# Block-diagonal gate products with the weight rows moving, turned back by transposes, in a two-layer hybrid block

## The chip, the cores and the metric

The kernel runs on one NeuronCore of a Trainium2 chip. The metric is the device time of one execution in microseconds (us). TensorE (PE in the rows, its weight loads PEld) multiplies, VectorE (DVE), ScalarE (ACT) and GpSimd (POOL) do the elementwise work, and SyncE (SP) issues the loads. A measurement is a set of executions on one chip, and its median is compared with that of the kernel before on the same chip.

## The reference, cut to what matters

A block of 256 tokens and width 2048 goes through a first layer (recurrence, attention, feed-forward, gated embedding) and two layers of a second kind. The change lies in the recurrence of the first layer:

```
D_RNN = 2816; N_RNN_BLOCKS = 16; RNN_BLOCK = 176
xb = x.reshape(B, S, N_RNN_BLOCKS, RNN_BLOCK)
r = sigmoid(einsum('bsnc,ncd->bsnd', xb, w_a).reshape(B, S, D_RNN) + b_a)
i = sigmoid(einsum('bsnc,ncd->bsnd', xb, w_x).reshape(B, S, D_RNN) + b_x)
log_a = -8 * r * softplus(-lam)
u = sqrt(-expm1(2 * log_a)) * (i * x)
h[t] = exp(log_a)[t] * h[t-1] + u[t]
```

Here x is the result of a causal convolution of width 4 over a projection of the input. The two gates r and i need a product with a block-diagonal matrix each: 16 blocks of 176x176. The chip works on 128 rows at a time, so the blocks do not fall on its boundaries.

## The kernel before, in words

All activations lie transposed: 128 features on the partitions, 256 tokens along the row. D_RNN is 22 such chunks ("m" in the code). All products are in float32 made of two float32r parts, a high and a low one: high times high, high times low, low times high.

**Weights.** All weights come from one stream, in tiles of eight 128x128 chunks (`G = 8`), in the order in which the program asks for them (`wnext`). `prep` issues a tile's load on SP, ScalarE copies its high part (`whi`, line 98 by way of `act`), VectorE subtracts for the low part (`wlo`, line 196). Four tiles of each part are held, so weights are prepared three tiles ahead (`LA = 3`).

**A projection** (`proj`, `mm3`) is 16 chunks of 128 input rows. The weight chunk is the stationary operand, the 256 tokens move; high and low part of the activation stand side by side, so a chunk is one matmul of 512 columns and one of 256 (lines 217, 218). `joined` adds the halves up: a ScalarE copy, then VectorE.

**The stage of the change.** A loop over m makes the projection for the recurrence (`xr_job`, with the convolution and its split into high and low part) and for its gelu gate (`gr_job`). When enough chunks are there, `rg_job` makes the two gate products of one output chunk: for both matrices, over the two to four input chunks that `rg_span` gives (70 in all for the 22 output chunks), three matmuls of 256 columns (lines 220 to 222): 22 jobs, 70 x 2 x 3 = 420 matmuls. Both gates share one PSUM bank of 512 columns (`pm`, tag "mm", four banks), which one ScalarE copy brings to SBUF. The weights come as zero-padded 128x128 chunks of the block-diagonal matrix. Four output chunks at a time go through `lru`: eight steps of pointwise work (sigmoid, tanh, exp, gelu, root, scan), queued as `sides`, of which the loop takes one after each projection or job. Behind the loop come the projections of a further gate (`gate_job`, m = 1 to 15), `flush` for steps that are left, and the product with `w_rnn_out`, which needs all 22 results.

**What sets the order.** TensorE's instructions run in the order in which the program writes them. A scheduler orders the other engines' instructions when the program is built; on each engine they then run strictly in that order, and an instruction that waits holds up those behind it. PSUM has eight banks: four with tag "mm", two "at" (`pa`), two "st" (`pst`). The tile `cs` holds constants, the identity among them, which line 810 to 812's transposes in a later layer use; it is loaded by line 560.

## Time and profile before

| | |
|---|---|
| median of 3 runs | 2869.33 us (2869.13 to 2869.34) |
| the profiled execution's own time | 2869.06 us |
| its span in the profile | 2866.9 us |
| granted TensorE clock, mean | 0.998 of full speed |

The span runs from the first to the last instruction; some 2 us around it belong to the execution's own time. "Busy" counts the time in which an engine has an instruction; matmuls overlap, so the distance from one start to the next is the price of a matmul, not its duration. A group of instructions is shown with its count, its busy time, the mean duration in ns, and the idle time of its engine just before it with what ended that. A timeline row has start, duration, engine, line, operation, output and inputs; `c`, `w` and `x` are tiles in SBUF, `pm`, `pa` and `pst` banks of PSUM, `raw` a weight tile as loaded.

### The profile page before, as it was taken

To read this page: it belongs to the slowest core of one execution; us is meant where nothing else is said; L and a number is where in the kernel's file an instruction comes from. 1 tells how busy PE (TensorE), PEld (TensorE's weight loads), DVE (VectorE), ACT (ScalarE), POOL (GpSimd) and SP (SyncE) were. 2 spreads that over 40 slices of the span, in tenths; PEclk is the share of its full clock that TensorE was granted. 3 is DMA by queue.
4 is the path that set the end of the run, shared out by engine and by line. 5 is a ranking of instruction groups with operands and counts; after the bars stand their busy time and mean duration, and the time that the engine had idled before them with its cause. 6 is when DMAs were issued, how large, how long until landed. Compare 5 with 4: busy or idle time off the path is not lost.

```text
span 2866.9 us, 43239 instructions
## 1 busy us (share of the span) xinstructions
PE 2846.1 (99%) x16414; PEld 2496.8 (87%) x16414; DVE 2018.1 (70%) x3306; ACT 1645.0 (57%) x2628; POOL 136.8 (5%) x155
## 2 busy tenths in 40 slices
PE   9999999999999999999999999999999999999997
PEld 8988888888888888888888888888888889888886
DVE  8788765666665776566565666776795688896676
ACT  6778764677765555544445455555464656554654
POOL 0112100111110000000000000000000001000000
PEclk9999999999999999999999999999999999999999
DMA  7565555545455556555555555655555555545553
GB/s 250 179 199 180 196 190 185 184 165 166 163 175 180 188 191 217 188 187 191 186 189 189 190 190 185 211 186 191 177 169 169 176 189 173 193 158 176 170 185 124
DMA packets 146433, 527.04 MB, mean 184 GB/s; under 512 B 16708, under 2 KB 17244, under 8 KB 146224
## 3 DMA queue, kind: packets, MB, share of 16 engines
q1 hardware_dynamic: 144720, 520.00, 54.8%
q0 software_dynamic: 1504, 4.29, 0.4%
q8 instruction: 128, 2.10, 0.3%
q14 instruction: 81, 0.66, 0.1%
HBM read 522.10 MB, written 4.47 MB: 184 GB/s over the span
## 4 chain that ended last, share of the span: by engine, by line
PE 99%; DVE 1%; DMA 0%; ACT 0%; SPq 0%; issue 0%; DVEq 0%
PE pm L217 55%; PE pm L218 28%; PE pm L290 3%; PE pm L289 3%; PE pm L291 3%; PE pm L221 2%; PE pm L220 2%; PE pm L222 2%; PE pa L795 0%; PE pa L819 0%; PE pa L598 0%; PE pa L796 0%; PE pa L619 0%; DVE x L1122 0%; DMA x<-xin_dram 0%; PE pa L217 0%
## 5 line engine op out<-in xcount | busy, mean ns | idle before, releaser
L217 PE MATMUL pm<-c,whi 128*128 128x512 f32 x6778 | 2382.6, 395 | 1.6 <-DVE c L355 1.6
L218 PE MATMUL pm<-c,wlo 128*128 128x256 f32 x6778 | 1898.5, 280 | 0.1
L196 DVE TENSOR_TENSOR wlo<-raw,whi 128x1024 fp32r<-128x1024 f32 (+1 forms) x984 | 1203.8, 1224 | 783.3 <-ACT whi L98 777.4
L98 ACT ACTIVATE whi<-raw 128x1024 fp32r<-128x1024 f32 (+1 forms) x984 | 1039.4, 1057 | 967.4 <-PE pm L217 500.4
L217 PEld LDWEIGHTS pm<-c,whi 128*128 128x128 f32 x6778 | 1273.1, 188 | 294.5 <-DVE c L355 1.9
L218 PEld LDWEIGHTS pm<-c,wlo 128*128 128x128 f32 x6778 | 1275.6, 188 | 0.8 <-DVE wlo L196 0.4
L98 ACT ACTIVATE c<-pm 128x256 f32<-128x256 f32 (+1 forms) x376 | 150.5, 402 | 110.7 <-PE pm L218 106.4
L98 ACT ACTIVATE c<-c 128x256 fp32r<-128x256 f32 (+2 forms) x357 | 139.2, 408 | 46.6 <-DVE c L450 24.9
L228 DVE TENSOR_TENSOR c<-pm,c 128x256 f32<-128x256 f32 x338 | 141.1, 418 | 4.5 <-ACT c L98 4.5
L289 PE MATMUL pm<-whi,c 128*128 128x512 f32 x320 | 126.9, 396 | 0.0
L290 PE MATMUL pm<-wlo,c 128*128 128x512 f32 x320 | 126.3, 395 | 0.0
L291 PE MATMUL pm<-whi,c 128*128 128x512 f32 x320 | 126.1, 394 | 0.0
L909 DVE SCALAR_TENSOR_TENSOR c<-w,sv,c 128x256 f32<-128x256 f32 x240 | 109.4, 497 | 0.8
L221 PE MATMUL pm<-c,whi 128*128 128x256 f32 (+1 forms) x377 | 106.4, 282 | 0.0
L220 PE MATMUL pm<-c,whi 128*128 128x256 f32 (+1 forms) x377 | 106.3, 282 | 0.0
L222 PE MATMUL pm<-c,wlo 128*128 128x256 f32 (+1 forms) x377 | 106.0, 281 | 0.0
L104 ACT ACTIVATE c<-c 128x256 f32<-128x256 f32 x219 | 85.5, 407 | 16.0 <-DVE c L228 14.1
L230 DVE TENSOR_TENSOR c<-c,c 128x256 f32<-128x256 f32 x176 | 75.8, 431 | 4.2
L291 PEld LDWEIGHTS pm<-whi,c 128*128 128x128 f32 x320 | 60.1, 188 | 14.2
L289 PEld LDWEIGHTS pm<-whi,c 128*128 128x128 f32 x320 | 60.1, 188 | 13.7
L290 PEld LDWEIGHTS pm<-wlo,c 128*128 128x128 f32 x320 | 60.1, 188 | 13.5
L220 PEld LDWEIGHTS pm<-c,whi 128*128 128x128 f32 x377 | 70.9, 188 | 0.9
(245 smaller groups left out, 1570.5 us busy)
## 6 DMA issues: line engine op xcount, KB each, us to landing
raw<-wst_dram SPq DMA_DIRECT2D x980, 512.0 KB, 3.3
scratch<-rows POOLq DMA_DIRECT2D x1, 2304.0 KB, 17.7
out_dram<-x SPq DMA_DIRECT2D x8, 256.0 KB, 2.0
x<-xin_dram SPq DMA_DIRECT2D x6, 256.0 KB, 7.7
c<-scratch POOLq DMA_DIRECT2D x12, 128.0 KB, 3.8
raw<-wst_dram SPq DMA_DIRECT2D x4, 256.0 KB, 4.0
sv<-vec_dram SPq DMA_DIRECT2D x1, 538.0 KB, 9.0
x<-xin_dram SPq DMA_DIRECT2D x4, 128.0 KB, 3.8
```

The lines of the kernel that those rows point to most:

```text
L98: return S.activation(o, i, func, **kw)
L196: V.tensor_tensor(lo[:, s], raw[:, s], h[:, s].bitcast(F32), op=OP.subtract)
L217: PE.matmul(o, wh, a[:, 0:512], start=first, stop=False)
L218: PE.matmul(o[:, 256:512], wl, a[:, 0:256], start=False, stop=last)
L220: PE.matmul(o, wh, a[:, 0:n], start=first, stop=False)
L221: PE.matmul(o, wh, a[:, n:2 * n], start=False, stop=False)
L222: PE.matmul(o, wl, a[:, 0:n], start=False, stop=last)
L228: V.tensor_tensor(t, o[:, 0:256], t, op=OP.add)
L289: PE.matmul(o, ah[:, tb], wh, start=first, stop=False)
L290: PE.matmul(o, ah[:, tb], wl, start=False, stop=False)
L291: PE.matmul(o, al[:, tb], wh, start=False, stop=last)
L909: V.scalar_tensor_tensor(a, pad[:, k:k + 256], wcol, a, op0=OP.mult, op1=OP.add)
```

## The change

The two gates' rows of one block now stand side by side as 352 columns and are the moving operand; the activation is the stationary one, in two halves of 128 tokens. `rg_block` works on one block of 176 instead of one output chunk of 128: for each of the two or three input chunks that the block touches, and for both token halves, three matmuls of 352 columns into two banks of tag "st". The result has tokens on the partitions. ScalarE copies it, cut at the boundaries of the 128-feature chunks, into one tile per chunk (`side_by`). `rg_turn` then turns a chunk back with four 128x128 transposes on TensorE (two gates, two token halves) into one bank of tag "at", and one ScalarE copy of 512 columns brings it to SBUF as before. A turn comes behind the next projection after its block. The constants with the identity are loaded with the vectors near the start; the gate projection m = 1 is put ahead of the last turns; the weight stream gets three-chunk requests that never cross a tile, with unused chunks where they would (7856 instead of 7852 chunks, 982 tiles of eight both times).

```diff
     def late_loads():
+        nc.sync.dma_start(cs, cst[:, :640])
         nc.sync.dma_start(sv, vec)
...
-    def rg_job(m):
-        span = rg_span(m)
-        both = pm(512)
-        for j, (key, d) in enumerate((("rg_a", rt), ("rg_x", it))):
-            proj(key, m, [xcs[k] for k in span], span, o=both[:, j * 256:(j + 1) * 256])
+    def rg_block(b):
+        span = block_span(b)
+        os = [pst(512) for _ in range(2)]
+        for kr in span:
+            ah, al = hl(xcs[kr])
+            wh, wl = (w[:, 0:2 * RNN_BLOCK] for w in wnext("rg", kr, b, 3))
+            first, last = kr == span[0], kr == span[-1]
+            for h, o in enumerate(os):
+                tb = slice(h * 128, (h + 1) * 128)
+                PE.matmul(o[:, 0:2 * RNN_BLOCK], ah[:, tb], wh, start=first, stop=False)
+                PE.matmul(o[:, 0:2 * RNN_BLOCK], ah[:, tb], wl, start=False, stop=False)
+                PE.matmul(o[:, 0:2 * RNN_BLOCK], al[:, tb], wh, start=False, stop=last)
+        for m in span:
+            if m not in side_by:
+                side_by[m] = slot()
+            lo, hi = max(b * RNN_BLOCK, m * 128), min((b + 1) * RNN_BLOCK, (m + 1) * 128)
+            to = side_by[m].rearrange("p (a h f) -> p a h f", a=2, h=2)
+            for h, o in enumerate(os):
+                with tc.high_priority():
+                    act(to[:, :, h, lo - m * 128:hi - m * 128],
+                        o[:, 0:2 * RNN_BLOCK].rearrange("p (a f) -> p a f", a=2)[:, :, lo - b * RNN_BLOCK:hi - b * RNN_BLOCK],
+                        AF.Copy)
...
+    def rg_turn(m):
+        s = side_by.pop(m)
+        both = pa(512)
+        for j in range(4):
+            PE.transpose(both[:, j * 128:(j + 1) * 128], s[:, j * 128:(j + 1) * 128], ident)
         t = slot()
         rt[m], it[m] = t[:, 0:256], t[:, 256:512]
         with tc.high_priority():
             act(t, both, AF.Copy)
...
     for m in range(KR):
         xr_job(m)
         side()
+        turn_to(ready)
         gr_job(m)
         side()
         if m == KR - 1:
             gate_job(0, COL_GA)
             side()
-        while ready < KR and rg_span(ready)[-1] <= m - min(2 if m < 4 else 1, KR - 1 - m):
-            rg_job(ready)
+        turn_to(ready)
+        while done < N_BLOCKS and block_span(done)[-1] <= m - min(2 if m < 4 else 1, KR - 1 - m):
+            rg_block(done)
             side()
...
+            done += 1
+        ready = KR if done == N_BLOCKS else done * RNN_BLOCK // 128
+    gate_job(1, COL_GA)
+    turn_to(KR)
+    order.extend([None] * (-len(order) % G))
...
-    for m in range(1, KD):
+    for m in range(2, KD):
         gate_job(m, COL_GA)
         side()
     flush()
...
-    nc.sync.dma_start(cs, cst[:, :640])
```

`turn_to(n)` turns the chunks up to n and queues `lru` for every four of them.

In the rows of the order that follow, the changed kernel's lines have their own numbers (L477 to L479 are the block products, L497 the transposes, L99 and L105 what L98 and L104 were).

**Order on TensorE, the seam of the last products.** Before, where the job of output chunk 19 ends and that of 20 begins (`pm_3437` and `pm_3470` are their banks, `c_` the split activation):

```order
L221 MATMUL pm_3437<-c_3142,whi_3377 128x256
L222 MATMUL pm_3437<-c_3142,wlo_3378 128x256
L220 MATMUL pm_3470<-c_3016,whi_3377 128x256 [waits PE_49]
L221 MATMUL pm_3470<-c_3016,whi_3377 128x256
L222 MATMUL pm_3470<-c_3016,wlo_3378 128x256
```

Now, where block 14 ends and block 15 begins (`pst_3452` and `pst_3453` are block 14's banks, `pst_3477` and `pst_3478` block 15's, in the same two places of PSUM):

```order
L479 MATMUL pst_3452<-whi_3384,c_3164 128x352
L477 MATMUL pst_3453<-whi_3384,c_3164 128x352
L478 MATMUL pst_3453<-wlo_3385,c_3164 128x352
L479 MATMUL pst_3453<-whi_3384,c_3164 128x352
L477 MATMUL pst_3477<-whi_3410,c_3164 128x352 [waits PE_49,Activation_49]
L478 MATMUL pst_3477<-wlo_3411,c_3164 128x352 [waits DVE_49]
L479 MATMUL pst_3477<-whi_3410,c_3164 128x352
L477 MATMUL pst_3478<-whi_3410,c_3164 128x352 [waits PE_49,Activation_49]
```

The products now wait for ScalarE at both of block 15's banks, which they did not at the seam before.

**Order on ScalarE, the same place.** Before, the copies of the jobs of chunks 19 to 21 out of their banks:

```order
L98 ACTIVATE c_3468<-pm_3437 128x512 [waits PE_49]
L104 ACTIVATE c_3468<-c_3468,sv 128x256 [waits Activation_49]
L104 ACTIVATE c_3468<-c_3468,sv 128x256
L98 ACTIVATE whi_3499<-raw_3497 128x1024 [waits DMAHW5_49,DVE_49,PE_49]
L98 ACTIVATE c_3489<-pm_3470 128x512 [waits PE_49,Pool_49]
L98 ACTIVATE c_3515<-pm_3496 128x512 [waits PE_49]
```

Now, the copies out of block 14's two banks (the sigmoids are those with `sv`):

```order
L99 ACTIVATE whi_3456<-raw_3454 128x1024 [waits DMAHW4_49,PE_49,Activation_49]
L99 ACTIVATE c_3448<-pm_3403 128x256 [waits PE_49,Activation_49]
L99 ACTIVATE c_3261<-pst_3452 128x2x96 [waits PE_49]
L99 ACTIVATE c_3474<-pst_3452 128x2x80 [waits Pool_49]
L105 ACTIVATE c_3346<-c_3346,sv 128x256 [waits Activation_49]
L99 ACTIVATE c_3261<-pst_3453 128x2x96 [waits PE_49]
L99 ACTIVATE whi_3481<-raw_3479 128x1024 [waits DMAHW5_49]
L99 ACTIVATE c_3474<-pst_3453 128x2x80
```

Where one copy freed a bank, there are two for each, and a weight copy stands between the two of the second bank.

**Order on ScalarE, the end of the gate projections.** Now, around the projections m = 14 and 15 (`pm_4239`, `pm_4291`); `c_4346` and `c_4351` are the high parts of the last two results of the recurrence:

```order
L105 ACTIVATE c_4178<-c_4178 128x256 [waits DVE_49]
L99 ACTIVATE whi_4294<-raw_4292 128x1024 [waits DMAHW2_49,PE_49]
L99 ACTIVATE c_4284<-pm_4239 128x256 [waits PE_49]
L105 ACTIVATE c_4178<-c_4178 128x256 [waits DVE_49]
L99 ACTIVATE c_4346<-c_3217 128x256 [waits DVE_49]
L101 ACT_TABLE_LOAD
L99 ACTIVATE whi_4316<-raw_4314 128x1024 [waits DMAHW3_49,PE_49]
L105 ACTIVATE c_3448<-c_3448 128x256
L99 ACTIVATE c_4351<-c_3217 128x256 [waits DVE_49,Activation_49]
```

The roots (the first and fourth row) stand on either side of the copy of projection 14, and both splits ahead of that of projection 15.

## Rows read from the trace of the kernel before

**Rows 1.** Page, parts 1 and 4: engines' busy time; the chain by engine.
```profile
PE 2846.1 (99%) x16414; PEld 2496.8 (87%) x16414; DVE 2018.1 (70%) x3306; ACT 1645.0 (57%) x2628; POOL 136.8 (5%) x155
...
PE 99%; DVE 1%; DMA 0%; ACT 0%; SPq 0%; issue 0%; DVEq 0%
```

**Rows 2.** Groups by line and shape, TensorE, 50 to 313 us.
```profile
L220 PE MATMUL pm<-c,whi 128*128 128x256 f32 x140 | 39.3, 281 | 0.0
```

**Rows 3.** Windows: busy us (count) by engine; then granted clock, DMA share, GB/s.
```profile
16.00:19.00 3.00, 3.00 (x19) 2.64 (x18) 3.00 (x7) 2.01 (x5) 0.00 (x0) 1.00 1.05 415
55.00:312.00 257.00, 257.00 (x1610) 231.23 (x1609) 212.90 (x345) 191.43 (x324) 39.30 (x36) 1.00 0.58 188
2079.00:2094.00 15.00, 15.00 (x92) 13.31 (x91) 14.74 (x40) 9.53 (x25) 0.00 (x0) 1.00 0.50 168
```

**Rows 4.** Groups by line and shape, ScalarE, 55 to 312 us.
```profile
L98 ACT ACTIVATE whi<-raw 128x1024 fp32r<-128x1024 f32 x92 | 96.7, 1054 | 31.5 <-PE pm L217 21.4 <-issue 5.6 <-ACT c L98 1.9
...
L104 ACT ACTIVATE c<-c,sv 128x256 f32<-128x256 f32 x40 | 18.2, 501 | 0.3
L98 ACT ACTIVATE c<-c 128x256 fp32r<-128x256 f32 x36 | 14.2, 410 | 30.3 <-DVE c L450 24.6 <-DVE c L509 5.6
L98 ACT ACTIVATE c<-pm 128x512 f32<-128x512 f32 x21 | 12.3, 585 | 0.9 <-PE pm L222 0.9
...
L98 ACT ACTIVATE c<-pm 128x256 f32<-128x256 f32 x21 | 7.6, 367 | 0.7 <-PE pm L218 0.7
```

**Rows 5.** Timeline of TensorE: first of the last 54 products, first matmul behind them.
```profile
305.78 0.28 PE L220 MATMUL pm<-c,whi 128*128 128x256 f32 x1
...
312.16 0.39 PE L217 MATMUL pm<-c,whi 128*128 128x512 f32 x1
```

**Rows 6.** Timeline of TensorE: first and twenty-eighth of a run with weights moving.
```profile
565.67 0.40 PE L289 MATMUL pm<-whi,c 128*128 128x512 f32 x1
...
571.95 0.39 PE L289 MATMUL pm<-whi,c 128*128 128x512 f32 x1
```

**Rows 7.** Timeline of TensorE: transposes of the later attention, then a projection.
```profile
2093.08 0.27 PE L810 MATMUL pa<-cs,w 128*128 128x128 f32 x1
2093.19 0.27 PE L811 MATMUL pa<-cs,w 128*128 128x128 f32 x1
...
2093.64 0.28 PE L218 MATMUL pm<-c,wlo 128*128 128x256 f32 x1
```

**Rows 8.** Timelines of ScalarE and TensorE: a weight copy's follower; a projection's end.
```profile
308.04 1.06 ACT L98 ACTIVATE whi<-raw 128x1024 fp32r<-128x1024 f32 x1 [1.49 <-issue]
309.00 0.58 ACT L98 ACTIVATE c<-pm 128x512 f32<-128x512 f32 x1
...
390.18 0.28 PE L218 MATMUL pm<-c,wlo 128*128 128x256 f32 x1
...
390.50 0.38 ACT L98 ACTIVATE c<-pm 128x256 f32<-128x256 f32 x1 [0.40 <-PE pm L218]
```

**Rows 9.** Timelines of SP, ScalarE and TensorE in the first 41 us.
```profile
15.00 0.33 SPq L376 DMA_DIRECT2D sv<-vec_dram  x1
...
25.45 1.04 ACT L98 ACTIVATE whi<-raw 128x1024 fp32r<-128x1024 f32 x1
...
30.88 0.39 ACT L98 ACTIVATE c<-pa 128x256 f32<-128x256 f32 x1 [1.01 <-PE pa L218]
...
34.51 0.20 ACT L98 ACTIVATE sp<-sv 128x22 f32<-128x22 f32 x1
...
40.26 0.70 PE L337 MATMUL pst<-c,onesD 128*128 128x256 f32 x2 [1.76 <-DVE c L384]
```

**Rows 10.** Timelines of POOL and VectorE: the last two columns' pointwise work.
```profile
370.95 2.10 POOL L504 TENSOR_TENSOR c<-c,c 128x256 f32<-128x256 f32 x2 [32.96 <-ACT c L104]
...
372.39 1.80 DVE L508 TENSOR_TENSOR_SCAN c<-c 128x256 f32<-128x256 f32 x2 [0.62 <-POOL c L504]
374.11 0.73 DVE L509 TENSOR_TENSOR c<-c,c 128x256 f32<-128x256 f32 x2
```

More of the change, by code (lines that the diff above doesn't have):

```diff
@@ L40 @@
 NW = 14
-N_CHUNKS = 7852
+N_CHUNKS = 7856
 NT = -(-N_CHUNKS // G)
@@ L67, with block_span @@
 NV = _vec_layout()
-def rg_span(m):
-    lo = (m * 128) // RNN_BLOCK * RNN_BLOCK
-    hi = min(((m * 128 + 127) // RNN_BLOCK + 1) * RNN_BLOCK, D_RNN)
-    return range(lo // 128, (hi - 1) // 128 + 1)
+N_BLOCKS = D_RNN // RNN_BLOCK
+def block_span(b):
+    return range(b * RNN_BLOCK // 128, (b * RNN_BLOCK + RNN_BLOCK - 1) // 128 + 1)
 @with_exitstack
@@ L201, in wnext @@
         t, c = divmod(i, G)
-        assert c + n <= G
+        if c + n > G:
+            order.extend([None] * (G - c))
+            t, c = t + 1, 0
         while state["prep"] <= min(t + LA, NT - 1):
@@ L206, in wnext @@
         for j in range(n):
-            order.append((key, kr, mc + j))
+            order.append((key, kr, (mc, j) if key == "rg" else mc + j))
         for old in [o for o in hi_t if o < t]:
@@ L460, in gr_job @@
             gr[m] = joined(o, "gr", R)
-    def rg_job(m):
-        span = rg_span(m)
-        both = pm(512)
-        for j, (key, d) in enumerate((("rg_a", rt), ("rg_x", it))):
-            proj(key, m, [xcs[k] for k in span], span, o=both[:, j * 256:(j + 1) * 256])
+    side_by = {}
+    def rg_block(b):
[20 more added lines that the diff above has]
+                        AF.Copy)
+        for k in [k for k in xcs if b + 1 == N_BLOCKS or k < block_span(b + 1)[0]]:
+            del xcs[k]
+    def rg_turn(m):
[3 more added lines that the diff above has]
+            PE.transpose(both[:, j * 128:(j + 1) * 128], s[:, j * 128:(j + 1) * 128], ident)
         t = slot()
@@ L470, in rg_job @@
             act(t, both, AF.Copy)
-        for k in [k for k in xcs if all(k not in rg_span(mm) for mm in range(m + 1, KR))]:
-            del xcs[k]
     at = {}
@@ L521, in gate_job, with turn_to @@
         gates[m] = joined(o, "gates", rr["R"])
-    ready, batch = 0, []
+    done, ready, turned, batch = 0, 0, 0, []
     first5 = proj("w_in", COL_XR + 2, ops)
     first6 = proj("w_in", COL_GR + 2, ops, hooks={6: token_scale})
+    def turn_to(n):
+        nonlocal turned, batch
+        while turned < n:
+            rg_turn(turned)
+            batch.append(turned)
+            turned += 1
+            if len(batch) == 4 or turned == KR:
+                lru(tuple(batch))
+                batch = []
     for m in range(KR):
@@ L1227, in _pack_weights @@
         mats[f"w_out_2_{i}"] = a["w_out_2"][i]
-    for key, name in (("rg_a", "w_rg_a"), ("rg_x", "w_rg_x")):
-        full = np.zeros((D_RNN, D_RNN), np.float32)
-        for b in range(D_RNN // RNN_BLOCK):
-            s = slice(b * RNN_BLOCK, (b + 1) * RNN_BLOCK)
-            full[s, s] = a[name][0, b]
-        mats[key] = full
-    w = np.zeros((NT, 128, G, 128), np.float32)
-    for i, (key, kr, mc) in enumerate(order):
+    rg = np.zeros((N_BLOCKS, D_RNN, 384), np.float32)
+    for b in range(N_BLOCKS):
+        rows = slice(b * RNN_BLOCK, (b + 1) * RNN_BLOCK)
+        rg[b, rows, 0:RNN_BLOCK] = a["w_rg_a"][0, b]
+        rg[b, rows, RNN_BLOCK:2 * RNN_BLOCK] = a["w_rg_x"][0, b]
+    w = np.zeros((NT, 128, G, 128), np.float32)
+    for i, item in enumerate(order):
+        if item is None:
+            continue
+        key, kr, mc = item
+        if key == "rg":
+            b, j = mc
+            w[i // G, :, i % G] = rg[b, kr * 128:(kr + 1) * 128, j * 128:(j + 1) * 128]
+            continue
         w[i // G, :, i % G] = mats[key][kr * 128:(kr + 1) * 128, mc * 128:(mc + 1) * 128]
```

6 lines of the change are left out of this document (1 added, 5 removed).

## The prediction, made before the result was known

> **What bounds the kernel now.** I read the page first, then the stage of the change by groups of lines and by windows, then single timelines for prices. TensorE is busy for 99% of the span, and the chain that ended last is TensorE in 99% of its length [rows 1]. So the time is a sum of TensorE's start-to-start distances, plus the few places where it waits. The products of the two gates are the 420 matmuls of lines 220 to 222 between 55 and 312 us: 140 of each line, each 128x256, no idle time before them; the row of line 220 stands for the three [rows 2]. In that stage TensorE is busy in all 257 us at a granted clock of 1.00, VectorE in 212.90 and ScalarE in 191.43 [rows 3]. The reader should note two things. A matmul's duration (281 ns) is not its price: the next one starts 0.12 us later. And ScalarE has 66 us without work there, partly spent waiting for VectorE's convolution (24.6 us) and for TensorE to free a weight buffer (21.4 us) [rows 4].
>
> **Removed.** The last 54 of the 420 run from 305.78 to 312.16, 0.1181 us each, without a gap between jobs [rows 5]. 420 x 0.1181 = **49.6 us** leave TensorE's path.
>
> **Added: the block products.** The 16 blocks touch 36 pairs of block and 128-row chunk (12 blocks two chunks, 4 blocks three); each pair has three products for each of two token halves, so 216 matmuls of 352 columns. No row has 352. With the weight rows moving, as here, 27 matmuls of 512 columns take 6.28 us from 565.67 to 571.95, 0.2326 each [rows 6]; 256 columns take 0.1181 [rows 5]. The bounds are 216 x 0.1181 = 25.5 and 216 x 0.2326 = 50.2 us. The distances of the two sizes are nearly in the ratio of their columns, so I take the line between them: 0.1181 + 96 x 0.1145/256 = 0.161, times 216 = **34.8 us**.
>
> **Added: the transposes.** 22 chunks x 4 = 88 of 128x128. The later attention has the same operation on the same type, also against the identity tile. Its three start 0.11 us apart, and from the first to the second matmul of the projection behind them pass 2093.64 - 2093.08 = 0.56 us, of which the projection's 512 columns are 0.233 [rows 7]. That is 0.109 each, start and change of operands included: 88 x 0.109 = **9.6 us** (bounds 9.4 to 9.8). Their duration stands as 0.27 us. The Trainium skill, "TensorE: Matmul & The Clock Gate", Part 4 (PE-mode transpose), gives about 275 ns for a transpose in a kernel and says that transposes do not count as activity for the clock. The rows agree with the duration, not with it as a price, and the granted clock around such groups is 1.00 [rows 3]. By that page's figure the 88 would be an estimated 24 us; it is the fourth rival below.
>
> The arithmetic of TensorE is then -49.6 + 34.8 + 9.6 = -5.2 us.
>
> **Added: ScalarE.** 72 copies out of the blocks' banks, 11264 columns in all. 256 columns cost 367 ns and 512 cost 585 [rows 4], so 0.15 + 0.00085 a column: 72 x 0.15 + 9.6 = 20.4 us. The 22 copies of 512 columns behind the transposes replace those behind the old products. ScalarE rises from 191 to 212 of some 252 us. Nearly everywhere this is hidden: a block's copies have a projection of 16 x 0.35 = 5.6 us before the turn that reads them. I add two waits where the orders show no cover.
>
> First, blocks 14 and 15 stand back to back and share the only two "st" banks. The first bank's last product of block 14 starts 8 x 0.161 = 1.29 us into it; a copy starts 0.32 us after the last matmul it waits for (390.18 to 390.50) [rows 8], and two copies of 192 and 160 columns follow each other in about 0.6. Block 15 is free to start at about 2.25 instead of 1.93: 0.3 us. Its second bank is due three matmuls later, at 2.7, but ScalarE has a sigmoid (0.50), a copy (0.27), a weight copy (0.96 to the next) and the last copy (0.29) in front [rows 4, 8]: 4.27, so 1.5 us. Together **1.8 us**. If the weight copy has its tile late, more; if ScalarE sorted itself otherwise, 0.
>
> Second, turns 19 to 21 follow each other on two "at" banks; turn 21 waits until the gate's copy and the first 512-column copy are done, 0.4 + 0.3 + 0.6 = 1.3 us after the gate, while two turns last 0.88: **0.5 us**.
>
> **Moved.** The constants (128 x 640 x 4 B = 0.33 MB) go in front of the vectors on SP's queue and in front of weight tile 8, at 15 us, where the DMA engines are saturated at 415 GB/s [rows 3, 9]: everything behind lands 0.8 us later. Tile 8's copy started at 25.45 and TensorE's first four projections end at about 30.6, just before the copy at 30.88 [rows 9]; the vectors are first read at 34.51. Nothing is priced. VectorE's sum that TensorE waits for at 40.26 [rows 9] stands behind the same instructions as before. At its old place the constants' load was hidden.
>
> One gate projection goes ahead of the last three turns, and the products' pointwise work starts a projection later, so of the last two columns' eight steps two are left for the flush behind gate 15. From the root's end a column needs POOL 1.05, the scan 0.9, a product 0.4 [rows 10], and the split's first half 0.41 [rows 4]; with as much for its second half 3.2 us, and w_rnn_out reaches columns 20 and 21 only 20 x 0.35 = 7 us after it starts. The order also has both splits before gate 15's copy. Nothing, with 3 us to spare; without that cover TensorE would wait inside the first w_rnn_out product. Weight tiles stay at 982 (7852 or 7856 chunks of eight to a tile), so copies, subtractions and loads for weights keep their number.
>
> **Sum.** -5.2 + 1.8 + 0.5 = -2.9 us. The profiled execution took 2869.06 us (span 2866.9), 0.27 below the median of 2869.33. So 2866.2 for such an execution and **2866.4 us** for the median. A measurement of this kernel tells 0.2%, 5.7 us, from no change: faster is below 2863.6, slower above 2875.1.
>
> **Rivals.**
> 1. *No new waits.* ScalarE's copies come in time everywhere: 2869.33 - 5.2 = 2864.1 us. For it: ScalarE's 66 us without work. Against: the two banks that blocks 14 and 15 share. To get below 2863.6 the 352-column product must also be 0.003 us cheaper than on my line, or some wait in the stage must go.
> 2. *ScalarE late, the slower side.* A block's copies queue behind a weight copy and pointwise work at each of the 16 blocks, and TensorE stands at the turn. If each costs one weight copy, 1.05 us, that is 16.8 us: 2883.2. It decides for slower from (2875.1 - 2866.4)/16 = 0.54 us a block. For it: 212 us of work, plus the 30 us in which ScalarE waits for VectorE [rows 4], is 242 of 252, so bursts have little room. Against: a turn comes 5.6 us after its block, and weights are prepared three tiles of 2.8 us ahead, so lateness must first pass several us.
> 3. *It saves nothing on the products*: a 352-column matmul costs as much as one of 512, 50.2 instead of 34.8: 2881.8. Against it: 256 and 512 differ by a factor of two.
> 4. *A transpose costs its duration*, 88 x 0.27 = 23.8 instead of 9.6: 2880.6. Against it: the distances in [rows 7].
>
> **How the numbers follow.** My forecast with single waits, 2864.5 to 2870, gets 0.55. Rival 1 gets 0.20, half of it below 2863.6. Rival 2 in small, 2870 to 2875.1, gets 0.08, in full 0.13; rivals 3 and 4 get 0.02 each. So faster 0.10, same 0.73, slower 0.17. The range leaves out half of what lies under 2863.6 and the slow cases: 2863.2 to 2874.0.
>
> **What would show it.** Right: 216 matmuls of 352 columns 0.16 us apart, 88 transposes 0.11 us apart, TensorE idle only between blocks 14 and 15 (about 1.8 us) and before turn 21 (0.5), and the first projection of w_rnn_out 3 us earlier than 396. Wrong: idle time before transposes all through the stage, released by ScalarE copies (rival 2); weight halves late to the projections; a distance of 0.23 (rival 3) or 0.27 (rival 4); a granted clock under 1.00 in the stage; or a new wait in the first 45 us behind the constants' load.

## The result, and the profile after

The changed kernel takes **2893.18 us** (median of 6 runs, 2888.77 to 2893.55) against 2869.39 us for the kernel before on the same chip: a ratio of 1.0076, interval 1.0066 to 1.0086. It is slower by 24 us, where I had forecast 3 us less. Two of the six runs were 3.3 and 4.4 us under the median, with a mean granted clock of 0.995 and 0.996 where the other four have 0.994. The profiled execution has a span of 2891.5 us.

The page of the changed kernel, its first part and the chain that ended last by engine; they answer to [rows 1]:

```profile
PE 2853.5 (99%) x16298; PEld 2497.5 (86%) x16298; DVE 2024.2 (70%) x3306; ACT 1633.6 (56%) x2700; POOL 132.7 (5%) x155
...
PE 89%; DVE 2%; ACT 1%; issue 0%; POOL 0%; DVEq 0%; ACTq 0%; POOLq 0%
```

The averages look untouched. What has changed is the chain, in which TensorE had 99% and now has 89%. The waits of TensorE say where: engine and line that wait, whom they wait for, us in total, times, longest.

```profile
PE pa L497 <- ACT c L99: 11.1, 6, 3.4
PE pst L477 <- ACT c L99: 4.5, 2, 4.0
...
PE pm L220 <- DVE c L311: 0.8, 2, 0.6
PE pa L852 <- DVE w L894: 0.8, 2, 0.4
```

Line 497 is the turns' transpose, line 477 the first product of a block. Together 15.6 us of new waits for ScalarE, where I had priced 2.3. The last two rows lie in later layers and are new as well.

**One wait followed back.** First TensorE around the longest wait before a turn, then ScalarE and VectorE at the same time (timelines: start, duration, engine, line, operation, result and operands, idle time before and who ended it):

```profile
145.01 0.32 PE L479 MATMUL pst<-whi,c 128*128 128x352 f32 x1
...
150.77 0.60 PE L497 MATMUL pa<-cs,c 128*128 128x128 f32 x4
154.81 1.18 PE L497 MATMUL pa<-cs,c 128*128 128x128 f32 x4 [3.44 <-ACT c L99]
```
```profile
151.14 0.72 ACT L99 ACTIVATE c<-c 128x256 fp32r<-128x256 f32 x2 [2.45 <-DVE c L454]
151.77 1.04 ACT L99 ACTIVATE whi<-raw 128x1024 fp32r<-128x1024 f32 x1
154.07 0.42 ACT L99 ACTIVATE c<-c 128x256 fp32r<-128x256 f32 x1 [1.26 <-DVE c L538]
154.39 0.87 ACT L99 ACTIVATE c<-pst 128x256 f32<-128x256 f32 x4
```
```profile
147.89 1.75 DVE L197 TENSOR_TENSOR wlo<-raw,whi 128x1024 fp32r<-128x1024 f32 x1
...
150.63 0.47 DVE L454 SCALAR_TENSOR_TENSOR c<-w,sv,c 128x256 f32<-128x256 f32 x1
151.03 1.21 DVE L197 TENSOR_TENSOR wlo<-raw,whi 128x1024 fp32r<-128x1024 f32 x1
...
152.84 0.68 DVE L537 TENSOR_TENSOR_SCAN c<-c 128x256 f32<-128x256 f32 x1
153.55 0.42 DVE L538 TENSOR_TENSOR c<-c,c 128x256 f32<-128x256 f32 x1
```

The block is complete at 145.3. A projection of 5.6 us follows, as planned, and TensorE is back for the second turn at 151.4. But the four copies out of the block's banks (`c<-pst`) start only at 154.39. ScalarE isn't busy: it stands idle for 2.45 us at the split of a convolution (line 454) and for 1.26 us at the split of the recurrence's product (line 538). VectorE comes late to both, because it subtracts weight tiles in between (the rows of line 197). The copies stand behind those splits on ScalarE, which works in order, and TensorE stands behind the copies.

**What a wait costs behind its end.** The windows of the changed kernel (busy time and count by engine, then granted clock, DMA share, GB/s) around the wait at the start and three of the longer new ones:

```profile
40.00:45.00 5.00, 4.25 (x17) 3.72 (x18) 3.17 (x16) 3.03 (x11) 0.00 (x0) 0.68 0.53 202
...
65.00:70.00 5.00, 2.95 (x15) 2.25 (x14) 4.53 (x15) 2.47 (x7) 0.00 (x0) 0.91 0.50 180
70.00:75.00 5.00, 5.00 (x23) 4.32 (x22) 2.00 (x3) 2.98 (x6) 0.72 (x1) 0.75 0.31 105
...
150.00:155.00 5.00, 1.56 (x11) 1.23 (x9) 4.96 (x9) 2.60 (x7) 0.00 (x0) 0.94 0.64 209
155.00:160.00 5.00, 5.00 (x23) 4.36 (x23) 4.29 (x9) 1.59 (x5) 0.00 (x0) 0.72 0.33 106
...
325.00:330.00 5.00, 3.28 (x10) 2.83 (x11) 3.21 (x4) 4.11 (x11) 1.61 (x2) 0.51 0.66 216
330.00:335.00 5.00, 5.00 (x25) 4.45 (x24) 1.23 (x1) 2.24 (x6) 0.26 (x1) 0.81 0.31 102
```

The granted clock, 1.00 all through the stage before [rows 3], falls to the lower level (1.2 of 2.4 GHz) in part of these stretches. There the same products stand further apart. TensorE's timeline, block 14 at the full clock and block 15 behind its wait:

```profile
320.13 0.32 PE L477 MATMUL pst<-whi,c 128*128 128x352 f32 x1
320.30 0.32 PE L478 MATMUL pst<-wlo,c 128*128 128x352 f32 x1
...
329.01 0.49 PE L477 MATMUL pst<-whi,c 128*128 128x352 f32 x1
329.31 0.49 PE L478 MATMUL pst<-wlo,c 128*128 128x352 f32 x1
```

0.17 us and 0.30 us. Over all stretches of 5 us from 30 to 420 us, one minus the granted clock sums to 2.04 (0 in the kernel before), that is 10.2 us lost at most, since some of the slow time lies in the waits themselves. Of these, 1.7 us stand at 40 to 50 us, behind the wait for VectorE at the start, which the kernel before has too [rows 9]; up to 8.5 us stand behind the new waits.

**The account.** As a mark between the stage and the later layers I take the start of the first product with `ones1r` (rows of the kernel before, then of the changed one, each with the last product with `onesD`):

```profile
536.26 0.28 PE L573 MATMUL pst<-c,ones1r 128*128 128x256 f32 x1
...
2850.75 0.61 PE L1129 MATMUL pst<-c,onesD 128*128 128x256 f32 x2
```
```profile
557.21 0.28 PE L615 MATMUL pst<-c,ones1r 128*128 128x256 f32 x1
...
2875.27 0.61 PE L1171 MATMUL pst<-c,onesD 128*128 128x256 f32 x2
```

The stage ends 20.95 us later; TensorE's arithmetic (-5.2), the new waits (15.6) and the clock (at most 10.2) give at most 20.6. From the first mark to the second pass 2318.06 us instead of 2314.49, so the later layers, whose products the change doesn't touch, lose another 3.57.

### The profile page after: what moved, and what is told of

Read it like the earlier page. It is cut to its first block, busy times and chain, and to the rows that moved or that the text cites. A ratio compares the mean times of both kernels' runs of the same rounds, so it can differ in the third digit from the quotient of the medians.

```text
span 2891.5 us, 43100 instructions
## 1 busy us (share of the span) xinstructions
PE 2853.5 (99%) x16298; PEld 2497.5 (86%) x16298; DVE 2024.2 (70%) x3306; ACT 1633.6 (56%) x2700; POOL 132.7 (5%) x155
## 4 chain that ended last, share of the span: by engine, by line
PE 89%; DVE 2%; ACT 1%; issue 0%; POOL 0%; DVEq 0%; ACTq 0%; POOLq 0%
PE pm L220 49%; PE pm L221 25%; PE pm L294 3%; PE pm L293 3%; PE pm L292 3%; PE pm L224 1%; PE pm L223 1%; PE pm L225 1%; DVE wlo L197 1%; ACT whi L99 0%; PE pa L837 0%; PE pa L861 0%; ACT c L99 0%; PE pa L640 0%; PE pa L661 0%
## 5 line engine op out<-in xcount | busy, mean ns | idle before, releaser
L99 ACT ACTIVATE whi<-raw 128x1024 fp32r<-128x1024 f32 (+1 forms) x984 | 1039.6, 1057 | 1078.1 <-issue 466.3
L220 PEld LDWEIGHTS pm<-c,whi 128*128 128x128 f32 x6778 | 1275.8, 188 | 297.5 <-DVE c L358 2.0
L99 ACT ACTIVATE c<-c 128x256 fp32r<-128x256 f32 (+2 forms) x357 | 140.2, 408 | 52.3 <-DVE c L233 20.3
L99 ACT ACTIVATE c<-pm 128x256 f32<-128x256 f32 (+1 forms) x354 | 133.6, 378 | 23.5 <-PE pm L221 19.4
L105 ACT ACTIVATE c<-c 128x256 f32<-128x256 f32 x219 | 84.2, 409 | 25.6 <-DVE c L231 22.7
L223 PE MATMUL pm<-c,whi 128*128 128x258 f32 (+1 forms) x237 | 67.2, 283 | 0.0
L224 PE MATMUL pm<-c,whi 128*128 128x258 f32 (+1 forms) x237 | 67.1, 283 | 0.0
L611 POOL TENSOR_TENSOR c<-c,c 128x256 fp32r<-128x256 f32 x40 | 39.6, 991 | 592.6 <-ACT c L99 585.8
L225 PE MATMUL pm<-c,wlo 128*128 128x258 f32 (+1 forms) x237 | 66.6, 281 | 0.0
```

The costliest lines, as they stand in the source:

```text
L99: return S.activation(o, i, func, **kw)
L220: PE.matmul(o, wh, a[:, 0:512], start=first, stop=False)
L223: PE.matmul(o, wh, a[:, 0:n], start=first, stop=False)
L224: PE.matmul(o, wh, a[:, n:2 * n], start=False, stop=False)
L225: PE.matmul(o, wl, a[:, 0:n], start=False, stop=last)
```

## Experiments

Theory A: copies stand behind splits that wait for VectorE, and the clock falls behind the waits. Rival B: ScalarE has too much work in any order. Rival C: the transposes cost more than their distance, or pull the clock down. Theories P, Q, L and those on the later layers came with the later runs. The table gives all 18 kernels; "stage" is the start of the first mark less 536.26, "later" the time between the marks less 2314.49, each from one profiled execution, so that a fall of the clock that happened in it (1.7 us or more) is in "stage".

| kernel | median us | ratio to before, interval | stage | later |
|---|---|---|---|---|
| the change | 2893.18 | 1.0076, 1.0066 to 1.0086 | +20.95 | +3.57 |
| e1_turn_later | 2884.68 | 1.0052, 1.0037 to 1.0067 | +8.76 | +6.64 |
| e2_seam | 2894.62 | 1.0085, 1.0068 to 1.0102 | +20.11 | +7.22 |
| e3_both | 2881.50 | 1.0040, 1.0025 to 1.0055 | +5.64 | +6.34 |
| e5_pool_splits | 2878.97 | 1.0030, 1.0018 to 1.0042 | +2.90 | +7.67 |
| e8_fill_seam | 2892.11 | 1.0081, 1.0065 to 1.0096 | +17.31 | +4.54 |
| e13_changed_no_gaps | 2882.26 | 1.0041, 1.0027 to 1.0055 | +11.46 | +2.46 |
| e7_all | 2871.86 | 1.0007, 0.9999 to 1.0016 | -4.20 | +6.76 |
| e12_all_again (e7) | 2871.66 | 1.0006, 0.9997 to 1.0015 | -3.91 | +6.75 |
| e11_turns_twice | 2877.08 | 1.0023, 1.0014 to 1.0033 | +5.72 | +2.88 |
| e9_no_gaps | 2868.91 | 0.9996, 0.9987 to 1.0005 | -3.51 | +3.30 |
| e14_no_gaps_plus8 | 2869.52 | 0.9999, 0.9991 to 1.0008 | -1.87 | +3.30 |
| e15_no_gaps_plus16 | 2869.74 | 1.0000, 0.9990 to 1.0009 | -2.97 | +3.30 |
| e17_no_gaps_slots5 | 2868.84 | 0.9996, 0.9987 to 1.0005 | -3.02 | +3.22 |
| e18_no_gaps_banks | 2869.08 | 0.9998, 0.9989 to 1.0007 | -3.11 | +3.29 |
| e4_load_first (before) | 2870.41 | 1.0003, 0.9995 to 1.0012 | +1.71 | +1.69 |
| e6_before_four_empty | 2873.82 | 1.0015, 1.0007 to 1.0024 | +2.68 | +3.86 |
| e10_before_eight_empty | 2868.11 | 0.9993, 0.9984 to 1.0001 | +0.83 | -0.93 |
| e16_before_slots | 2871.63 | 1.0005, 0.9997 to 1.0014 | +0.39 | +1.68 |

### More cover for the copies

**e1_turn_later**: the changed kernel, a turn comes behind two projections, not one.

```diff
         side()
-        turn_to(ready)
         gr_job(m)
```


> Edit: a turn comes behind two projections after its block (11.2 us) instead of one (5.6 us); all else as in the changed kernel. Theory A (TensorE waits at the turns because the copies out of the blocks' banks stand on ScalarE behind splits that wait for VectorE, up to 3.4 us too late, and the clock falls after the longer waits): the 11.1 us of waits before transposes nearly vanish and with them about 5 us of half clock (65 to 75, 150 to 160, 265 to 275 us); the wait of 4.5 us between blocks 14 and 15 stays: 2893.2 - 16 = 2877, between 2874 and 2880. Rival B (ScalarE has too much work in the stage, so lateness only moves on): waits of 8 us or more stand elsewhere, at the weight halves or the later turns, and the time stays above 2885. Rival C (the transposes themselves cost more than 0.11 us or pull the clock down): no change beyond 2 us, 2891 to 2895.

**e2_seam**: the changed kernel, the last gate projection of the loop moved between blocks 14 and 15.

```diff
-        if m == KR - 1:
-            gate_job(0, COL_GA)
...
             done += 1
+            if done == N_BLOCKS - 1:
+                gate_job(0, COL_GA)
```


> Edit: the gate projection m = 0 stands between blocks 14 and 15 instead of ahead of both, so that the two banks have 5.6 us to be emptied; all else as in the changed kernel. Theory A: the 4.5 us of waits at the seam go and with them about 3.4 us of half clock (325 to 335 us), the waits at the turns stay: 2893.2 - 8 = 2885, between 2882 and 2888. Rival B: the wait appears at the last turns instead, above 2890. Rival C: no change, 2891 to 2895.

**e3_both**: both edits.


> Edits of e1_turn_later and e2_seam together. Theory A: no wait over 1 us is left in the stage and the clock stays at full; the sum of TensorE's work stands (-5.2 us on the kernel before), with 0 to 4 us more in the later layers, whose order the scheduler has changed: 2864 to 2869. Rival B: 2875 or more, with waits for ScalarE at other places. Rival C: 2883 or more, with a granted clock under 1.00 around the transposes.

The waits of e1, then of e3:

```profile
PE pst L477 <- ACT c L99: 5.4, 1, 5.4
PE pm L221 <- DVE wlo L197: 2.9, 3, 2.3
...
PE pa L497 <- ACT c L99: 0.9, 1, 0.9
```
```profile
PE pst L477 <- ACT c L99: 3.4, 1, 3.4
PE pm L221 <- DVE wlo L197: 2.6, 2, 2.3
...
PE pa L497 <- ACT c L99: 0.9, 1, 0.9
```

With 11 us of cover the turns' waits fall from 11.1 to 0.9 us, and the stage ends 12.2 us earlier. ScalarE's work is the same, so its amount isn't what TensorE waited for there: B is weakened. It isn't out by this: e1's 2884.68 is above Theory A's range and just under the 2885 of B, because 8.3 us of waits stand elsewhere (5.4 before block 15, where it was 4.5, and 2.9 for VectorE's halves of weight tiles) and the later layers lose 3.1 us more than the change's. e2 was a miss: block 15 still waits 3.71 us behind the gate projection, and the time is no better than the change's. Both edits together take half of the loss away, and miss Theory A's range too: 2881.50 is in B's. What is left in the stage is one wait of 3.4 us before a block and a new one of 2.3 for VectorE's half of a weight tile; the later layers lose 6.34 us.

### Taking the splits off both engines

**e5_pool_splits**: the changed kernel; POOL makes both halves of the splits of the convolution and of the recurrence's result.

```diff
+    def split_pool(src):
+        w = slot(F32R)
+        h, lo = hl(w)
+        nc.gpsimd.tensor_copy(h, src)
+        nc.gpsimd.tensor_tensor(lo, src, h.bitcast(F32), op=OP.subtract)
+        return w
...
-        xc[m], xcs[m] = c, split(c)
+        xc[m], xcs[m] = c, split_pool(c)
...
-                yr[m] = split(gr[m])
+                yr[m] = split_pool(gr[m])
```


> Edit: the splits of the convolution's result and of the recurrence's result into high and low part go to POOL, both halves (it is 5% busy); turns and seam as in the changed kernel. ScalarE then has no instruction in the stage that waits for VectorE's scan product or convolution, and 36 copies less. Theory A: the copies out of the banks run when their products are done, the waits at the turns fall from 11.1 to under 2 us, the seam to the 1.8 us of the prediction or less: 2866 to 2873. Rival B (load): ScalarE loses 14 of some 212 us, so waits fall by a third at most: 2884 to 2890. Rival C: 2890 or more. If POOL is too slow for the splits (0.8 to 1.5 us each half), TensorE waits at block products for the low part of the convolution instead.

The waits of e5:

```profile
PE pm L221 <- DVE wlo L197: 1.9, 4, 0.7
PE pa L504 <- ACT c L99: 1.9, 2, 0.9
...
PE pst L484 <- ACT c L99: 0.5, 1, 0.5
```

Without the turns being moved, the waits for ScalarE shrink from 15.6 to 2.4 us, and from 50 us to the stage's end the clock stays at 1.00. The stage ends 18 us earlier than the change's. B had given the waits a third less at most; with the instructions on which ScalarE waited for VectorE gone, they are 13.2 us less. The edit lightens ScalarE as well and gives it another order, so it does not speak against B by itself; together with e1 it does. The whole time, 2878.97, is above Theory A's 2866 to 2873, since the later layers lose 7.67 us.

### The clock and the transposes

**e8_fill_seam**: the changed kernel; products that nobody reads fill the wait before block 15.

```diff
+        if b == N_BLOCKS - 1:
+            spare, (fill, _) = pm(512), hl(xcs[span[0]])
+            for j in range(26):
+                PE.matmul(spare[:, 0:256], fill[:, 0:128], fill, start=True, stop=True)
         os = [pst(512) for _ in range(2)]
```


> The changed kernel with 26 products of 256 columns whose result nobody reads, ahead of the last block, where TensorE waits 4.0 us for ScalarE; by 0.117 us each they take 3.0 of these 4.0 us. Theory A (the clock falls because of the wait, and its fall costs 3.4 us at this place, from granted clocks of 0.51 and 0.81 in two stretches of 5 us): the granted clock stays at 1.00 there, and the time is 2.5 to 3.5 us less than the changed kernel's, 2889.7 to 2890.7. Rival C (the clock falls because of the blocks and transposes themselves, or its fall costs nothing since TensorE waits anyway): 2893 +- 1.

Windows of e8 at the filled wait; behind them, the first turn's wait and the window behind it:

```profile
325.00:330.00 5.00, 4.00 (x24) 3.58 (x24) 2.34 (x4) 4.31 (x10) 1.88 (x2) 1.00 0.59 210
330.00:335.00 5.00, 4.29 (x28) 3.65 (x26) 2.55 (x3) 2.73 (x4) 0.00 (x0) 1.00 0.39 120
```
```profile
66.17 0.82 PE L501 MATMUL pa<-cs,c 128*128 128x128 f32 x4 [2.04 <-ACT c L99]
...
70.00:75.00 5.00, 5.00 (x32) 4.60 (x31) 2.94 (x4) 3.73 (x9) 0.73 (x1) 1.00 0.58 181
```

The clock held at the filled wait. Across it the products gain 1.8 us on the changed kernel's (1.88 us ahead before it, 3.64 behind it), less than the expected 2.5 to 3.5: 1.9 us of waiting remain beside the filling, and in the changed kernel some of the slow time lay in the wait itself. The median is 1.1 us lower, but the two kernels' intervals cover each other, so the whole time shows nothing here; the trace does. In it the fall goes with the idle time, not with the blocks. And in e7 and e9 (below), with the same blocks and transposes and no wait of TensorE over 1 us in the stage behind the one at the start, the granted clock is 1.00 from 30 to 420 us. C falls for the clock.

The second fence is a comparison that I hadn't planned: the wait of 2.04 us before the first turn is as long as in the changed kernel (2.05), but here the clock stays at 1.00, and the products, 1.49 us ahead of the changed kernel's before it, are 3.05 us ahead once that kernel's fall is over. Behind the next wait, 3.44 us in both, e8 loses 3.4 us to the clock and the changed kernel 1.7. Equal waits need not cost the same; the windows of the changed kernel show the fall at the first turn (0.91 and 0.75).

**e11_turns_twice**: e7 (below), each of the 88 transposes issued twice into the same place.

```diff
-        for j in range(4):
+        for j in (0, 1, 2, 3, 0, 1, 2, 3):
```


> The kernel with all the edits (splits on POOL, turns later, gate between the last two blocks, 7860 chunks, 2871.9 us) with every transpose of the turns issued twice into the same place: 88 more. My prediction's price, the distance of 0.109 us: 9.6 us more, 2881.5 +- 1.5. Rival C (a transpose holds TensorE for its duration of 0.27 to 0.29 us, or draws the clock down): 24 us more or above, 2895 or later.

The stage ends 9.92 us later than e7's, 0.113 us a transpose; my price was 0.109. (A wait of 0.9 us is gone and one of 0.4 has come, so a transpose may cost 0.118.) The whole time rises by only 5.2 us and misses the 2880 to 2883 that I expected, because the later layers of this program lose 3.9 us less. With 176 transposes the granted clock is 1.00 in every stretch of 5 us from 30 to 420 us. C falls altogether.

### The stage with all edits

**e7_all**: the splits on POOL, turns later, gate between the blocks, and padding behind the stage that puts the later weights at the places within their tiles that they have in the kernel before.

```diff
-    order.extend([None] * (-len(order) % G))
+    order.extend([None] * ((4 - len(order)) % G))
```


> The changed kernel with the splits of the convolution and of the recurrence on POOL, the turns two projections later, the gate between the last two blocks, and the padding behind the recurrence chosen so that the later layers' weights stand where they stand in the kernel before. Theory A with P: the stage keeps TensorE's own saving of 5.2 less waits of 2 to 4 us, and the later layers lose nothing: 2865 to 2870. Rival B (ScalarE's work is too much for the stage in any order): the waits come back at other places, 2875 or more. Rival Q (the later loss doesn't depend on the places in the tiles): 2872 to 2877.

```profile
PE pa L504 <- ACT c L99: 0.9, 1, 0.9
PE pm L273 <- ACT c L99: 0.2, 1, 0.2
```

Of the stage's waits for ScalarE one of 0.9 us is left, and the stage ends **4.20 us ahead** of the kernel before. My arithmetic with this wait gives -5.2 + 0.9 = -4.3. The saving on TensorE is real; but the later layers lose 6.76, and the whole is 2 us above the kernel before (1 is just inside the interval) and above the range of Theory A.

**e13_changed_no_gaps**: the changed kernel alone, with single chunks filling the places that a triple leaves free at a tile's end, and no padding (7820 chunks).

```diff
-        i = len(order)
+        if n == 1 and holes:
+            i = holes.pop(0)
+        else:
+            c = len(order) % G
+            if c + n > G:
+                holes.extend(range(len(order), len(order) + G - c))
+                order.extend([None] * (G - c))
+            i = len(order)
+            order.extend([None] * n)
...
```


> The changed kernel with one edit: the gaps of the weight stream filled and no padding, 7820 chunks, so that the later layers' weights stand where they stand in the kernel before. Theory A with P: the turns' waits (11.1 us in six) and the last block's (4.5) stay with their falls of the clock, so the stage still stands 17 to 22 us behind; the four later jumps of together 2.2 us are gone: 2887 to 2892. Rival (the gaps and the tiles loaded for them made the waits): turns' waits under 6 us, 2882 or less.

```profile
PE pa L505 <- ACT c L99: 6.1, 6, 2.4
PE pst L485 <- ACT c L99: 4.4, 1, 4.4
```

My theory missed here, and the rival's numbers nearly came out (6.1 us for under 6, 2882.26 for 2882 or less): 36 chunks less, four and a half tiles of splitting on ScalarE and VectorE, take 5.0 us off the turns' waits and 5.1 off the clock's loss, 1.7 of it at the start (falls are left at 65 to 75 and 315 to 325 us only). So the gaps had a share of the waits. Whether by the work they add or by where they put the weight tiles in the queues was not tried apart.

**e9_no_gaps**: e7 with the gaps filled in the same way.


> The kernel of the last study but one place (splits on POOL, turns two projections later, the gate between the last two blocks), with the gaps of the weight stream filled: single chunks of the next projections take the places that a triple leaves free at a tile's end, so 7820 chunks in place of 7860, and the later layers' weights keep their places in the tiles. That kernel stood 4.2 us ahead of the kernel before at the end of the stage and lost 6.9 us in the later layers without a wait, by distances between matmuls 0.002 us longer. Theory R (that slow loss hangs on which of the rotating buffers the later layers' tiles fall into, and so changes with the count of tiles before them): the stage's 4 to 5 us stay, the later loss is anywhere from -1 to 7 us, 2864 to 2872. Rival S (the slow loss follows from the splits on POOL or from the reordered work): 2871 to 2873 as before. A stage that loses its 4 us would say that the free places make TensorE wait for tiles that come later, since the preload is one tile shorter while a place is open.

2868.91 against 2870.22 us: with e17, its near copy, the fastest kernel with the new products, and not told apart from the kernel before.

### The later layers

**e4_load_first**: the kernel before with only the constants' load moved.

```diff
     def late_loads():
+        nc.sync.dma_start(cs, cst[:, :640])
```


> The kernel before with one edit: the load of the constants stands ahead of the load of the vectors, as in the change. Theory A (all of the stage's loss is ScalarE's order and the clock behind it; the load is free, as I predicted): 2869.4 +- 1, and no stretch after 40 us with a granted clock under 1. Rival L (the moved load costs: it delays the vectors, the wait for VectorE at 46 us grows, the clock falls there, and work behind the recurrence comes later): 2871 to 2877, with a granted clock of about 0.68 in 40 to 45 us as the changed kernel shows it.

No difference that can be told, as priced. The fall of the clock that Rival L expects is there in the profiled execution, 0.68 in 40 to 45 us behind the start's wait of 1.62 us. But the moved load isn't what it takes: e6 (below) keeps the load at its old place and has the fall too, behind a wait of 1.76 us:

```profile
40.00:45.00 5.00, 3.64 (x16) 3.17 (x17) 3.54 (x17) 2.81 (x10) 0.00 (x0) 0.79 0.73 254
```

**e6_before_four_empty** and **e10_before_eight_empty**: the kernel before with four or eight empty chunks behind the recurrence.

```diff
+    order.extend([None] * 4)
     for m in range(1, KD):
```


> The kernel before with one edit: four empty chunks in the weight stream behind the recurrence, so that the later layers' weights stand at the same places of the eight-chunk tiles as in the changed kernel. In the traces of the four variants of the changed kernel, the later layers lost another 3.7 to 7.6 us after the recurrence was over, in the same four jumps (0.4, 0.5, 0.55, 0.7 us) and in slow drifts. Theory P (that loss comes from the shifted places in the tiles): 2872 to 2877, with the four jumps at 1009, 2079, 2537 and 2761 us of the kernel before. Rival Q (it comes from what the recurrence leaves behind, or from the order of the loads): 2869.4 +- 1 and no jumps.

> The kernel before with eight empty chunks behind the recurrence: the later layers' weights keep their places within the tiles, and each tile falls into the next buffer. Theory P (only the place within a tile matters): 2869.7 +- 1, no jumps, plus at most 0.3 for one more tile to be split. Theory R (the buffer matters too): a slow loss in the later layers without waits and without the four jumps, 2871 to 2876.

The waits of e6 that the kernel before doesn't have:

```profile
PE pm L217 <- DVE c L308: 0.8, 2, 0.6
PE pa L811 <- DVE w L853: 0.8, 2, 0.4
```

They are the same four places and sizes as in the changed kernel's first fence of waits; with the slower start behind each they make jumps of 0.49, 0.61, 0.60 and 0.85 us. Four empty chunks cost 4.2 us in a kernel in which nothing else was changed; eight cost nothing (2868.11, even 0.6 us under Theory P's range). P is shown for these jumps, 2.6 us together. The rest of e6's later loss, 1.3 us, comes without waits.

**The slow rest.** e7 and e9 have no such jumps and still lose 6.76 and 3.30 us, without a wait, by distances between matmuls that are some 0.001 us longer (e7: 2.5 us over 2,286 matmuls between 1200 and 1600 us). Six runs went after it: e7 once more; e9 with eight or sixteen empty chunks; and, in the kernel before (e16) and in e9 (e17, e18), these lines behind the recurrence, the first two taking operand buffers, the others result banks:

```diff
+    for _ in range(5):
+        nc.gpsimd.memset(slot()[:, 0:1], 0.0)
...
+    spare = [pm() for _ in range(4)]
+    for p in spare[::-1]:
+        V.memset(p[:, 0:1], 0.0)
```

> The kernel with all the edits and 7860 chunks (2871.86 us; 4.20 us ahead of the kernel before at the first product with ones1r, then 6.76 us of loss in the later layers, no waits of note there) once more, unchanged. Theory K (the slow later loss belongs to the kernel: its tiles, buffers and order): later loss 6.8 +- 0.7, stage -4.2 +- 0.5, 2871.9 +- 1. Theory X (it belongs to the execution or the chip): a later loss that differs by 2 us or more, while the stage stays at -4.2.

> The kernel with all the edits and without gaps (2868.91 us; stage 3.51 us ahead of the kernel before, then a later loss of 3.30 us) with eight empty chunks behind the recurrence: every later tile keeps its inner places and falls into the next of the rotating buffers. Theory R (the slow later loss hangs on the buffers): stage -3.5 +- 0.5, later loss differing from 3.30 by over 1 us in either direction; with the change that the same eight chunks made in the kernel before (0.9 us gained in the later layers) 2864 to 2869. Rival S (it follows from the reordered work alone): later loss 3.3 +- 0.5, 2869 +- 1.

> The same with sixteen empty chunks, two buffers on. Theory R: a third value of the later loss, different from the other two by over 0.5 us. Rival S: 3.3 +- 0.5, 2869 +- 1. In both, two more tiles to split (2.1 us of ScalarE, 2.5 us of VectorE) stand behind the stage, where the kernel before has no wait.

> The kernel before with five more operand buffers taken (and one column of each cleared on POOL) behind the recurrence: in the later layers the same 13,053 TensorE products stand in the same order with the same weights, weight buffers and result banks, but some 2,000 of them read their other operand from another of the 51 buffers. Theory O (the slow later loss hangs on where the operands lie): later loss differs from 0 by over 1 us, either way, 2867 to 2875. Theory M (it hangs on the order of the result banks, which the changed kernel has turned round against the kernel before): later loss 0 +- 1.0, 2869.9 +- 1.

> The kernel with all the edits and without gaps (2868.91 us, later loss 3.30 us in three executions of three kernels with the same operand buffers and banks) with the same five operand buffers taken. Theory O: later loss differs from 3.30 by over 1 us. Theory M: 3.3 +- 0.5.

> The kernel with all the edits and without gaps, with four result banks taken and given back behind the recurrence: the later products keep their operands' and weights' buffers and their order, and half of them write to another bank. Theory O: later loss 3.3 +- 0.5. Theory M: it differs from 3.30 by over 1 us; with the loss gone 2865 to 2867, ahead of the kernel before by more than the measurement.

e12 repeats e7's later loss to 0.01 us: it belongs to the kernel. e14 puts all later weights into other buffers, e15 three quarters of them, e18 9,410 of the 13,053 results into other banks: 3.30, 3.30 and 3.29, so neither matters. Other operand buffers moved the kernel before by 1.68 us (e16) and e9 by only 0.08 (e17). The 13,053 products are the same in the same order in all of these programs.

e17's 0.08 looks like a run against the operands' places, but it is a sum. The first mark and the same later product, some 1,420 us behind it, in e9, e14 and e17:

```profile
532.75 0.28 PE L628 MATMUL pst<-c,ones1r 128*128 128x256 f32 x1
...
1952.80 0.40 PE L228 MATMUL pm<-c,whi 128*128 128x512 f32 x1
```
```profile
534.39 0.28 PE L629 MATMUL pst<-c,ones1r 128*128 128x256 f32 x1
...
1954.44 0.40 PE L228 MATMUL pm<-c,whi 128*128 128x512 f32 x1
```
```profile
533.24 0.28 PE L630 MATMUL pst<-c,ones1r 128*128 128x256 f32 x1
...
1951.91 0.40 PE L228 MATMUL pm<-c,whi 128*128 128x512 f32 x1
```

That is 1420.05, 1420.05 and 1418.67 us. Followed product by product, e14, e15 and e18 stay within 0.003 us of e9 over all later layers, and e12 within 0.004 of e7. e17 is up to 1.38 us ahead of e9 and later up to 0.31 behind it. As programs, e16 and the kernel before, and e17 and e9, have the same order on every engine but for the five clears on POOL; behind the mark they differ in the buffers alone, in some 1,500 and 1,300 operand reads of the products and in what the other engines read and write there. e4's products, too, keep order, weight buffers and banks and have some 2,000 operand reads moved, and its later loss is 1.69. So where the operands lie changes the slow rest, and weight buffers and result banks do not. By what mechanism it does so, and which places are good, stays open.

## Why the prediction was wrong

**TensorE's terms held.** The products of 352 columns stand 0.16 us apart (0.161 taken), a transpose costs 0.113 (0.109), and the stage without waits gains what the sum said, 4.20 for 4.3. Rivals 3 and 4 are out, and with rival 4 the page's figure as a price: "TensorE: Matmul & The Clock Gate", Part 4 of the Trainium skill, gives some 275 ns, and the rows agree with that as a duration only (273 ns on average in e7).

**The step that failed** is "Nearly everywhere this is hidden: a block's copies have a projection of 16 x 0.35 = 5.6 us before the turn that reads them." I compared ScalarE's added work with its free time. The free time was not free: part of it stands in front of the copies, because ScalarE waits in it, in order, for VectorE. The row that says so was in my own table, a split `c<-c` with 24.6 and 5.6 us of idle time before it [rows 4]. I used it in rival 2 as 30 us of load and did not ask which instructions queue behind a wait. At 145 us the copies were 9.1 us behind the block, and 5.6 were planned. What the runs showed in its place are 15.6 us of waits at seven places: with 11.2 us of cover (e1) those before turns fall from 11.1 to 0.9, and without the splits on ScalarE (e5) all fall to 2.4. The gaps in the weight stream had a share as well, 5.0 us of the turns' waits (e13), and I had priced them at nothing because the count of tiles stays; how the gaps act stays open.

**Rival 2 had the right place**, TensorE standing at the turn behind late copies, with a chance of 0.21. Its price of 16.8 us is near the 15.6 measured by luck: not a weight copy at each of 16 blocks, but 0.8 to 4.5 us at seven places. Two terms were missing from every case. The clock, up to 10.2 us: I took 1.00 for granted in the stage, and listed a lower clock only among the signs of being wrong. And the later layers, 3.6 us: "Weight tiles stay at 982 ..., so copies, subtractions and loads for weights keep their number" is true, but their places within the tiles shift by four chunks, which alone makes four jumps of 2.6 us together (e6), and the change moves operand buffers as well, on which the slow rest hangs (e16, e17).

**The wait between blocks 14 and 15** was seen, at 1.8 us; it is 4.5 (and turn 21's is 0.9 for 0.5), and e2 shows that a projection in between does not cover it: on ScalarE, splits that wait 2.15 and 1.56 us for VectorE stand in front of these copies too (319.54 and 323.14 us in the changed kernel's timeline). My list of what stands in front had ScalarE's work alone. "Nothing is priced" for the moved load held: e4 is 0.75 us over the kernel before, with 1 inside the interval.

## What to carry to other kernels

Before a new copy is called hidden by an engine's idle time, look at what the engine is idle for: a wait of an in-order engine stands in front of everything behind it, and idle time of that kind is queue, not room. A wait on TensorE is to be priced with what the clock can take behind it, here up to 8.5 us on 15.6. And a change that alters the number of chunks in a shared weight stream moves the tile boundaries of all later layers: pad it to the old places first, or the comparison measures that too. When two totals agree, follow the products in between: e17's total hid a difference of over 1 us.

## What the hardware showed

TensorE's granted clock fell to the lower level behind waits of 1.62 (changed kernel), 1.76 (e6), 2.05 and 2.25 (changed kernel), 2.32 (e3), 3.44, 4.00 (changed kernel), 4.38 (e13) and 5.42 us (e1), each time for 1.7 or 3.4 us of lost time. It did not fall behind waits of 1.62 (e7), 1.76 (kernel before, [rows 9]), 2.04 (e8), 2.31 (e1) and 2.37 us (e13). With 26 products that nobody reads in the wait of 4.00 us it stayed at 1.00 there (e8).

Kernels with the same 13,053 later products in the same order take from 0.9 us less to 7.7 us more for them than the kernel before (6.8 more without a single new wait), and the one that was run again repeats its value. Programs whose later products differ only in weight buffers or result banks agree within 0.003 us over some 2,300 us; programs that differ only in operand buffers do not (e16, e17).
